# Two more weight slots and a column-grouped router in a hybrid encoder layer with 16 experts

## The chip, the cores and the metric

The kernel runs on one core of a Trainium2 chip. The metric is the device time of one execution in microseconds (us). A core has TensorE (matrix products, results in PSUM), VectorE, ScalarE and GpSimd (element-wise work), SyncE (here it issues nearly all transfers) and 16 DMA engines that move data between HBM and the core's SBUF. SBUF has 128 partitions; a slot of 8 KB in each of them holds 1 MB.

## The reference

One layer on 256 tokens of width 2048, all in float32. The first sub-layer is not changed. The second routes: each of 16 experts chooses the 32 tokens with the highest affinity to it.

```python
h = h + merged @ w_out[l]
h = h + expert_choice_ffn(rms_norm(h, ffn_norm_g[l]), w_router[l], w_gate_e[l], w_up_e[l], w_down_e[l])

def expert_choice_ffn(hn, w_router, w_gate_e, w_up_e, w_down_e):
    cap = CAPACITY_FACTOR * T // N_EXPERTS                      # 32
    aff = jax.nn.softmax((hn @ w_router).astype(jnp.float32), axis=-1)
    gate, idx = lax.top_k(aff.transpose(0, 2, 1), cap)
    xe = jax.vmap(lambda h, i: h[i])(hn, idx)
    hid = jax.nn.silu(einsum(xe, w_gate_e)) * einsum(xe, w_up_e)   # 2048 -> 1024
    ye = einsum(hid, w_down_e) * gate[..., None]                   # 1024 -> 2048
    out = zeros.at[idx].add(ye)
```

The expert weights are 3 x 16 x 2048 x 1024 x 4 bytes, 402.7 MB, of the 556 MB that the kernel moves.

## The kernel before

The order of the work is: normalisation of x; the input projection and the RWKV-7 heads, interleaved; the attention projections (`da`) and attention; the two branch projections (`br`), merged into mh and ml; the output projection (`w_out`); the routing; and four quarters of four experts each. Each engine runs its instructions in an order fixed at build time by a scheduler, which takes the program's order, priorities and a timing model; semaphores hold the engines together.

**Projections.** `wsplit` (L198) loads a chunk of weights of 0.5 MB into one of three raw buffers, ScalarE casts it to a high part wh (L205) and VectorE subtracts to a low part wl (L206), two buffers each. `project_t` (L213) multiplies: 12 matmuls of 512 columns for each chunk (L224 to L226). w_out is four blocks of 512 output columns, 8 chunks each, 32 chunks in all. A chunk's transfer is issued when the chunk three before it is split.

**The expert loads.** 384 loads of 1 MB stand in the list ew_loads, for every quarter 64 of gate and up weights and 32 of down weights, in the order in which they are used. `fetch` (L171) takes the next load and a slot from the pool that slot_of (L165) names, and issues its transfer on SyncE (L179). The slots: NEW = 14 form the ring, of which NE1 = 2 lie in pool ew1 (open since the attention projections) and 12 in ewa, opened ahead of w_out; NEB = 8 more (ewb, L887) are opened after the routing code and hold one load each, loads 14 to 21, until the first quarter's gate and up products are done; their place then goes to the accumulator acc. `pace` (L188), called with each chunk, issues one load for every PACE = 3 chunks while ring slots are free; a one-element GpSimd copy (L176) ties it to the chunk's split. What is left of the 14 goes out behind w_out (L831). All other loads wait for a slot that TensorE has done with.

**Memory.** Pools are stacked from the left and from the right end of SBUF. On the left, mg holds mh and ml (32 KB a partition) and wp the raw, wh and wl buffers; both are released after w_out, and ewb takes their place and more. On the right lie hres, ew1, ewa and, during w_out only, out2 (o2, L810) with hT and hsq. A pool that is opened over memory of an earlier one waits until that one's tiles are done with.

**Router logits.** For each w_out block, h is completed (L817), transposed in PSUM (pth, L821) and copied to hT (L822), 512 features by 256 tokens. Then 8 products with hT as the stationary operand (128x128) and 16 columns of wr as the moving one give the block's share of the logits, plg (L826), and VectorE adds it to lgt (L828, L830). A float32 product appears as two matmul records. After the last block come the norm (hrs), the softmax, the transposed affinities, four rounds of top-8, the one-hot matrices oh and ohr, the gather of the tokens (pxe, L906, xe, L907) and the first expert matmuls (pgu, L923): four experts at a time, each in its own group of 32 columns of the array. Down products are pd (L957).

Of the kernel before, what the change touches and what calls it, by code (L numbers as in the profile page):

```python
# [8 lines left out]
F32 = mybir.dt.float32  # L9
# [3 lines left out]
OP = mybir.AluOpType  # L13
AX = mybir.AxisListType
# [4 lines left out]
T = 256  # L19
# [5 lines left out]
NE = 16  # L25
# [7 lines left out]

GSCHED = (1, 4, 1, 4, 6)
PS, PCH = 9000, 16000
NEW, NE1, NEB = 14, 2, 8
PACE = 3

C_ID = 0
C_ROPE = C_ID + 128  # L40
# [12 lines left out]
def trunk_kernel(ctx, tc, x, attn_norm_g, w_in, q_norm_g, k_norm_g, lambda_q1, lambda_k1, lambda_q2,  # L53
# [3 lines left out]
    nc = tc.nc  # L57
    V, A, G, PE, SP = nc.vector, nc.scalar, nc.gpsimd, nc.tensor, nc.sync
    left = "left"
# [5 lines left out]
    lp = tc.alloc_tile_pool(name="lp", bufs=1, space=PSUM)  # L65
# [5 lines left out]
    @contextmanager  # L71
    def prio(base):
        old = tc.cur_priority
        if base > 0:
            tc.cur_priority = base
        yield
        tc.cur_priority = old if base > 0 else tc.cur_priority

    def misc(shape, name):
        return prepp.tile(shape, F32, name=name, tag="pr")  # L80

    cst = cp.tile([128, C_RW], F32, name="cst")
    ident = cst[:, C_ID:C_ID + 128]
# [68 lines left out]
    for q in range(4):  # L152
# [4 lines left out]
        for c0, w in pieces(q):  # L157
            n = 2048 // w
            for c in range(8 // n):
                for j in range(4):  # L160
                    ew_loads.append(w_down_e[0, 4 * q + j].rearrange("(p ft) n -> p ft n", ft=8)
                                    [:, n * c:n * c + n, c0:c0 + w])
    ew_state = dict(pools=[None, None, None], tiles=[], used=0, chunks=0)

    def slot_of(i):  # L165

        if NEW <= i < NEW + NEB:
            return 2
        return int((i if i < NEW else i - NEB) % NEW >= NE1)

    def fetch(after=None):  # L171
        i = len(ew_state["tiles"])
        pool = ew_state["pools"][slot_of(i)]
        w = pool.tile([128, 2, FF], F32, name="w", tag="w")
        if after is not None:
            G.tensor_copy(w[0:1, 0, 0:1], after)  # L176
        src = ew_loads[i]
        w = w.rearrange("p a f -> p (a f)").rearrange("p (a f) -> p a f", f=src.shape[2])
        SP.dma_start(w, src)  # L179
        ew_state["tiles"].append(w)  # L180
# [7 lines left out]
    def pace(wl):  # L188
# [4 lines left out]
        ew_state["chunks"] += 1  # L193
        if ew_state["chunks"] % PACE == 0:
            with prio(2000000 + ew_state["chunks"]):
# [446 lines left out]
    hres = tc.alloc_tile_pool(name="hres", bufs=1, side=right)  # L642
    hrow = hres.tile([128, 2, D], F32, name="h")
    fg = hres.tile([128, KT], F32, name="fg")
    wr = hres.tile([128, KT, NE], F32, name="wr")
    fg2 = hres.tile([16, 128], F32, name="fg2")
    ssb = hres.tile([128, 2, 4], F32, name="ssb")
    lgt = hres.tile([128, 2, NE], F32, name="lgt")
# [24 lines left out]
    with ExitStack() as es:  # L673
# [59 lines left out]
        for t in range(2):  # L733
            SP.dma_start(hrow[:, t], x[0, t * 128:(t + 1) * 128, :])
        SP.dma_start(fg, ffn_norm_g[0].rearrange("(p kt) -> p kt", kt=KT))
        SP.dma_start(wr, w_router[0].rearrange("(kt p) e -> p kt e", p=128))
        SP.dma_start(fg2, ffn_norm_g[0].rearrange("(a b) -> a b", b=128))
        for h in range(8):
# [23 lines left out]
            for t in range(2):  # L762
                for j in range(2):
                    PE.matmul(po[:, t], aT[:, j, t * 128:(t + 1) * 128], vt[:, j, h * 128:(h + 1) * 128],
                              start=j == 0, stop=j == 1)
# [42 lines left out]
    w_out_k = w_out[0].rearrange("(kt p) n -> p kt n", p=128)  # L808
    with ExitStack() as es:
        o2 = es.enter_context(tc.tile_pool(name="out2", bufs=2, side=right))  # L810
        for blk in range(4):
            cs = slice(blk * 512, (blk + 1) * 512)
            ps = project_t(w_out_k, KT, blk * 512, mh, ml, f"wo{blk}", (chp, "ch") if blk % 2 else None)
            hT = o2.tile([128, 4, T], F32, name="hT", bufs=1)
            hsq = o2.tile([128, 512], F32, name="hsq", bufs=1)
            for t in range(2):
                V.tensor_tensor(h[:, t, cs], ps[t], h[:, t, cs], op=OP.add)  # L817
                A.activation(hsq, h[:, t, cs], AF.Square, accum_out=ssb[:, t, blk:blk + 1])
                pt = misc([128, 4, 128], f"pth{blk}_{t}")
                for j in range(4):  # L820
                    PE.transpose(pt[:, j], h[:, t, blk * 512 + j * 128:blk * 512 + (j + 1) * 128], ident)  # L821
                A.copy(hT[:, :, t * 128:(t + 1) * 128], pt)  # L822
            pl = misc([128, 2, NE], f"plg{blk}")
            for t in range(2):
                for j in range(4):
                    PE.matmul(pl[:, t], hT[:, j, t * 128:(t + 1) * 128], wr[:, blk * 4 + j], start=j == 0, stop=j == 3)  # L826
            if blk == 0:
                V.tensor_copy(lgt, pl)  # L828
            else:
                V.tensor_tensor(lgt, pl, lgt, op=OP.add)  # L830
    while len(ew_state["tiles"]) < NEW:  # L831
        fetch()
    mg.release()
# [50 lines left out]


    with ExitStack() as es:
        ewb = tc.alloc_tile_pool(name="ewb", bufs=NEB, side=left)  # L887
        ew_state["pools"][2] = ewb
        for q in range(4):
            es_ = slice(4 * q, 4 * q + 4)  # L890

# [31 lines left out]
                                PE.matmul(pgu[2 * gu + hf][js], xe[kt // 4][:, kt % 4, js],  # L923
                                          wt[2 * j + gu][:, k, hf * 512:(hf + 1) * 512], start=kt == 0, stop=kt == KT - 1)
            if q == 0:
                ewb.release()
                e3 = es.enter_context(tc.tile_pool(name="e3", bufs=1, side=left))
                acc = e3.tile([128, 2, D], F32, name="acc")
            gT = e3.tile([128, T], F32, name="gT")
# [11 lines left out]
            hT = e3.tile([128, 8, 128], F32, name="hdT", bufs=1)  # L941
# [5 lines left out]
            for c0, cw in pieces(q):  # L947
# [3 lines left out]
                for c in range(8 // nft):  # L951
                    wt = [expert_w() for j in range(4)]
                    for k, nb, j in ([(k, 0, j) for j in range(4) for k in range(nft)] if nft == 8 else
# [4 lines left out]
                                          start=ft == 0, stop=ft == 7)  # L958
# [61 lines left out]
```

## Time and profile before

| what | value |
|---|---|
| three runs | 1873.23, 1873.61, 1876.11 us; median 1873.61 |
| the profiled execution | 1877.81 us, span of its instructions 1876.0 us |
| busy in the span | TensorE 1679.5 us (90%), its weight loads 1032.0, VectorE 701.4, ScalarE 440.4, GpSimd 189.9 |
| DMA | 556.48 MB, mean 297 GB/s |
| granted TensorE clock | 0.977 of full speed on average |

A row of the profile names the line of the kernel, the engine, the operation and the tiles (out<-in, with shapes as partitions x elements). PE is TensorE's matmuls, PEld its weight loads, SPq SyncE's queue of transfers. "idle before" is what the engine waited for ahead of the instruction. The chain of waits follows the work that ended last back to its start. A DMA share of 1 means that all 16 engines were busy; values a little over 1 occur. Some matmul records are missing from a trace, so counts of merged rows can be low.

### The profile page before, as it was taken

Reading aid. Unit: us, or ns where it says so; the run is one execution under the profiler, and the core shown is the slowest. Engines: PE = TensorE matmul, PEld = TensorE weight load, DVE = VectorE, ACT = ScalarE, POOL = GpSimd, SP = SyncE. Lnnn points to the kernel's source line nnn. Section 1 sums busy time; section 2 is a strip of 40 time slices with the busy share of each in tenths; the row PEclk is TensorE's granted clock in tenths of the full one; section 3 lists DMA queues with packets and bytes.
Section 4 is the critical chain, followed back from the end, with each engine's and each line's share of the span. In section 5 each row is a group of like instructions: output and inputs, shape, how many; then the busy total and the mean of one; then the engine's idle time right before and its main releaser. Section 6 shows DMA issues by size and latency. Waiting matters only on the chain.

```text
span 1876.0 us, 27452 instructions
## 1 busy us (share of the span) xinstructions
PE 1679.5 (90%) x11179; PEld 1032.0 (55%) x11179; DVE 701.4 (37%) x1524; ACT 440.4 (23%) x768; POOL 189.9 (10%) x295
## 2 busy tenths in 40 slices
PE   7999999998998999999989889888898888878878
PEld 6988898887996778998734222222222222211223
DVE  4678797877645667774410000000000000000000
ACT  6444443443434455444300000000000000000000
POOL 2342223322001331000000000000000000000000
PEclk9999999999999999999989999999999999999999
DMA  5655644554657565788799999999999999999997
GB/s 170 172 141 146 171 112 117 135 142 115 170 153 234 169 201 162 221 261 298 275 419 393 424 421 425 427 427 425 420 425 427 427 424 420 425 427 427 425 417 278
DMA packets 230382, 556.48 MB, mean 297 GB/s; under 512 B 40954, under 2 KB 138736, under 8 KB 197232
## 3 DMA queue, kind: packets, MB, share of 16 engines
q1 hardware_dynamic: 229904, 554.68, 79.8%
q8 instruction: 88, 1.44, 0.3%
q14 instruction: 38, 0.31, 0.0%
q0 software_dynamic: 352, 0.05, 0.0%
HBM read 543.14 MB, written 11.53 MB: 296 GB/s over the span
## 4 chain that ended last, share of the span: by engine, by line
DMA 35%; PE 27%; SPq 2%; DVE 1%; issue 1%; ACT 0%; POOL 0%; ACTq 0%; POOLq 0%; DVEq 0%
DMA w<-in_w_down_e_dram 13%; DMA w<-in_w_gate_e_dram 11%; DMA w<-in_w_up_e_dram 11%; PE pgu L923 6%; PE pd L957 4%; SPq L179 2%; PE pxe L906 2%; PE pc_br L242 2%; PE pc_br L244 2%; PE pj_wo L225 2%; PE pc_br L243 2%; PE pj_wo L226 2%; PE pj_wo L224 2%; PE pj_da L225 1%; PE pj_da L224 1%; PE pj_da L226 1%
## 5 line engine op out<-in xcount | busy, mean ns | idle before, releaser
L923 PE MATMUL pgu<-w,xe 128*32 128x512 f32 x2048 | 458.6, 610 | 63.4 <-DMA w<-in_w_gate_e_dram 31.6
L923 PEld LDWEIGHTS pgu<-w,xe 128*32 128x32 f32 x2048 | 111.9, 110 | 393.9 <-issue 232.6
L957 PE MATMUL pd<-w,hdT 128*32 128x512 f32 (+1 forms) x1088 | 246.3, 589 | 54.7 <-DMA w<-in_w_down_e_dram 53.8
L957 PEld LDWEIGHTS pd<-w,hdT 128*32 128x32 f32 x1088 | 65.2, 111 | 232.4 <-DMA w<-in_w_down_e_dram 122.3
L242 PE MATMUL pc_gt<-xh,wh_gt 128*128 128x256 f32 x512 | 149.9, 295 | 1.4 <-ACT wh_gt L205 1.4
L244 PE MATMUL pc_gt<-xh,wl_gt 128*128 128x256 f32 x512 | 145.6, 295 | 2.7 <-DVE wl_gt L206 2.5
L243 PE MATMUL pc_gt<-xl,wh_gt 128*128 128x256 f32 x512 | 148.0, 292 | 0.0
L938 ACT ACTIVATE th<-pgu 128x512 f32<-128x512 f32 x8 | 4.8, 597 | 522.1 <-PE pgu L923 522.1
L907 DVE TENSOR_TENSOR xe<-pxe,fg 128x512 f32<-128x512 f32 x16 | 11.0, 690 | 296.4 <-PE pgu L923 241.3
L242 PE MATMUL pc_rkv<-xh,wh_rkv 128*128 128x256 f32 x384 | 111.4, 293 | 1.0 <-ACT wh_rkv L205 1.0
L244 PE MATMUL pc_rkv<-xh,wl_rkv 128*128 128x256 f32 x384 | 108.1, 293 | 3.9 <-DVE wl_rkv L206 3.9
L243 PE MATMUL pc_rkv<-xl,wh_rkv 128*128 128x256 f32 x384 | 110.4, 290 | 0.0
L966 DVE TENSOR_TENSOR acc<-poe,acc 128x512 f32<-128x512 f32 (+1 forms) x26 | 16.9, 651 | 245.3 <-PE poe L965 245.3
L242 PEld LDWEIGHTS pc_gt<-xh,wh_gt 128*128 128x128 f32 x512 | 100.0, 195 | 4.6 <-ACT wh_gt L205 1.6
L243 PEld LDWEIGHTS pc_gt<-xl,wh_gt 128*128 128x128 f32 x512 | 100.1, 195 | 2.3 <-issue 1.2
L244 PEld LDWEIGHTS pc_gt<-xh,wl_gt 128*128 128x128 f32 x512 | 97.4, 195 | 6.1 <-DVE wl_gt L206 3.9
L939 DVE SCALAR_TENSOR_TENSOR th<-th,pgu 128x512 f32<-128x512 f32 x8 | 5.5, 688 | 252.0 <-ACT th L938 251.9
L206 DVE TENSOR_TENSOR wl_gt<-raw_gt,wh_gt 128x1024 fp32r<-128x1024 f32 x64 | 80.4, 1256 | 39.5 <-ACT wh_gt L205 39.3
L205 ACT CAST wh_gt<-raw_gt 128x1024 fp32r<-128x1024 f32 x64 | 67.0, 1046 | 92.8 <-PE pc_gt L243 75.8
L225 PE MATMUL pj_da<-wl_da,xh 128*128 128x512 f32 x192 | 77.8, 405 | 7.0 <-DVE wl_da L206 6.9
L961 ACT COPY ye<-pd 128x512 f32<-128x512 f32 (+1 forms) x17 | 9.5, 560 | 310.0 <-PE pd L957 310.0
L206 DVE TENSOR_TENSOR wl_da<-raw_da,wh_da 128x1024 fp32r<-128x1024 f32 x48 | 63.7, 1326 | 34.3 <-ACT wh_da L205 33.4
(385 smaller groups left out, 2868.0 us busy)
## 6 DMA issues: line engine op xcount, KB each, us to landing
w<-in_w_gate_e_dram SPq DMA_DIRECT2D x128, 1024.0 KB, 19.5
w<-in_w_up_e_dram SPq DMA_DIRECT2D x128, 1024.0 KB, 19.5
w<-in_w_down_e_dram SPq DMA_DIRECT2D x128, 1024.0 KB, 18.1
raw_gt<-in_w_in_dram SPq DMA_DIRECT2D x64, 512.0 KB, 3.8
raw_rkv<-in_w_in_dram SPq DMA_DIRECT2D x48, 512.0 KB, 3.8
raw_da<-in_w_in_dram SPq DMA_DIRECT2D x48, 512.0 KB, 3.6
raw_wo<-in_w_out_dram SPq DMA_DIRECT2D x32, 512.0 KB, 5.3
raw_br<-in_w_branch_b_dram SPq DMA_DIRECT2D x16, 512.0 KB, 4.1
```

The source lines that it names most:

```text
L179: SP.dma_start(w, src)
L205: A.copy(wh[:, :n], raw[:, :n])
L206: V.tensor_tensor(wl[:, :n], raw[:, :n], wh[:, :n].bitcast(F32), op=OP.subtract)
L224: PE.matmul(ps[t], lh[:, kt, s], wh[:, j], start=first, stop=False)
L225: PE.matmul(ps[t], lh[:, kt, s], wl[:, j], start=False, stop=False)
L226: PE.matmul(ps[t], ll[:, kt, s], wh[:, j], start=False, stop=last)
L242: PE.matmul(ps[c][:m], wh[:, j, cs], rh[:, kt], start=first, stop=False)
L243: PE.matmul(ps[c][:m], wh[:, j, cs], rl[:, kt], start=False, stop=False)
L244: PE.matmul(ps[c][:m], wl[:, j, cs], rh[:, kt], start=False, stop=last)
L906: PE.matmul(px[:, j], h[:, t, kt::KT], ohr[:, t], start=t == 0, stop=t == 1)
L923: PE.matmul(pgu[2 * gu + hf][js], xe[kt // 4][:, kt % 4, js], wt[2 * j + gu][:, k, hf * 512:(hf + 1) * 512], start=kt == 0, stop=kt == KT - 1)
L957: PE.matmul(pd[nb][js], hT[:, ft, js], wt[j][:, k, nb * nw:(nb + 1) * nw], start=ft == 0, stop=ft == 7)
```

## The change

Five edits:

- NEW becomes 16 and PACE 2: the ring has 16 slots (14 in ewa), and among the w_out chunks one load is issued for every two chunks.
- The 8 late slots come from two pools, 6 and 2, opened one after the other on the left; slot_of gives loads 16 to 21 to the first and 22 and 23 to the second.
- The DMA scratch, memory at the start of SBUF for the descriptors of transfers that GpSimd issues, is set to 2048 bytes a partition (default 16384).
- Router logits: the 16 columns of wr become the stationary operand and hT (256 tokens) the moving one. The four 128-feature pieces of a block go to four column groups of the array, that is to partitions 0, 32, 64 and 96 of one PSUM tile plg, and accumulate there over the four blocks. plg is zeroed first, since only 16 of each 32 partitions are written.
- At the end plg is copied to SBUF (lgs, in out2), multiplied with rsum (the identity summed over its four pieces, made once) so that the four groups are added and the result is transposed to tokens on partitions, and copied to lgt.

```diff
--- before.py
+++ after.py
@@ -33,8 +33,8 @@
 
 GSCHED = (1, 4, 1, 4, 6)
 PS, PCH = 9000, 16000
-NEW, NE1, NEB = 14, 2, 8
-PACE = 3
+NEW, NE1, NEB = 16, 2, (6, 2)
+PACE = 2
 
 C_ID = 0
 C_ROPE = C_ID + 128
@@ -160,13 +160,13 @@
                 for j in range(4):
                     ew_loads.append(w_down_e[0, 4 * q + j].rearrange("(p ft) n -> p ft n", ft=8)
                                     [:, n * c:n * c + n, c0:c0 + w])
-    ew_state = dict(pools=[None, None, None], tiles=[], used=0, chunks=0)
+    ew_state = dict(pools=[None, None, None, None], tiles=[], used=0, chunks=0)
 
     def slot_of(i):
 
-        if NEW <= i < NEW + NEB:
-            return 2
-        return int((i if i < NEW else i - NEB) % NEW >= NE1)
+        if NEW <= i < NEW + sum(NEB):
+            return 2 + (i >= NEW + NEB[0])
+        return int((i if i < NEW else i - sum(NEB)) % NEW >= NE1)
 
     def fetch(after=None):
         i = len(ew_state["tiles"])
@@ -643,6 +643,7 @@
     hrow = hres.tile([128, 2, D], F32, name="h")
     fg = hres.tile([128, KT], F32, name="fg")
     wr = hres.tile([128, KT, NE], F32, name="wr")
+    rsum = hres.tile([128, 32], F32, name="rsum")
     fg2 = hres.tile([16, 128], F32, name="fg2")
     ssb = hres.tile([128, 2, 4], F32, name="ssb")
     lgt = hres.tile([128, 2, NE], F32, name="lgt")
@@ -733,6 +734,7 @@
         for t in range(2):
             SP.dma_start(hrow[:, t], x[0, t * 128:(t + 1) * 128, :])
         SP.dma_start(fg, ffn_norm_g[0].rearrange("(p kt) -> p kt", kt=KT))
+        V.tensor_reduce(rsum, ident.rearrange("p (j e) -> p e j", j=4), axis=AX.X, op=OP.add)
         SP.dma_start(wr, w_router[0].rearrange("(kt p) e -> p kt e", p=128))
         SP.dma_start(fg2, ffn_norm_g[0].rearrange("(a b) -> a b", b=128))
         for h in range(8):
@@ -808,6 +810,9 @@
     w_out_k = w_out[0].rearrange("(kt p) n -> p kt n", p=128)
     with ExitStack() as es:
         o2 = es.enter_context(tc.tile_pool(name="out2", bufs=2, side=right))
+
+        plg = lp.tile([128, T], F32, name="plg", tag="L")
+        V.memset(plg, 0.0)
         for blk in range(4):
             cs = slice(blk * 512, (blk + 1) * 512)
             ps = project_t(w_out_k, KT, blk * 512, mh, ml, f"wo{blk}", (chp, "ch") if blk % 2 else None)
@@ -820,14 +825,14 @@
                 for j in range(4):
                     PE.transpose(pt[:, j], h[:, t, blk * 512 + j * 128:blk * 512 + (j + 1) * 128], ident)
                 A.copy(hT[:, :, t * 128:(t + 1) * 128], pt)
-            pl = misc([128, 2, NE], f"plg{blk}")
-            for t in range(2):
-                for j in range(4):
-                    PE.matmul(pl[:, t], hT[:, j, t * 128:(t + 1) * 128], wr[:, blk * 4 + j], start=j == 0, stop=j == 3)
-            if blk == 0:
-                V.tensor_copy(lgt, pl)
-            else:
-                V.tensor_tensor(lgt, pl, lgt, op=OP.add)
+            for j in range(4):
+                PE.matmul(plg[32 * j:32 * j + NE], wr[:, blk * 4 + j], hT[:, j], start=blk == 0, stop=blk == 3)
+        lgs = o2.tile([128, T], F32, name="lgs", bufs=1)
+        V.tensor_copy(lgs, plg)
+        pl = misc([128, 2, NE], "pl")
+        for t in range(2):
+            PE.matmul(pl[:, t], lgs[:, t * 128:(t + 1) * 128], rsum[:, 0:NE], start=True, stop=True)
+        V.tensor_copy(lgt, pl)
     while len(ew_state["tiles"]) < NEW:
         fetch()
     mg.release()
@@ -884,8 +889,8 @@
 
 
     with ExitStack() as es:
-        ewb = tc.alloc_tile_pool(name="ewb", bufs=NEB, side=left)
-        ew_state["pools"][2] = ewb
+        ewb = [tc.alloc_tile_pool(name=f"ewb{i}", bufs=n, side=left) for i, n in enumerate(NEB)]
+        ew_state["pools"][2:] = ewb
         for q in range(4):
             es_ = slice(4 * q, 4 * q + 4)
 
@@ -923,7 +928,8 @@
                                 PE.matmul(pgu[2 * gu + hf][js], xe[kt // 4][:, kt % 4, js],
                                           wt[2 * j + gu][:, k, hf * 512:(hf + 1) * 512], start=kt == 0, stop=kt == KT - 1)
             if q == 0:
-                ewb.release()
+                for z in ewb[::-1]:
+                    z.release()
                 e3 = es.enter_context(tc.tile_pool(name="e3", bufs=1, side=left))
                 acc = e3.tile([128, 2, D], F32, name="acc")
             gT = e3.tile([128, T], F32, name="gT")
@@ -1006,7 +1012,7 @@
     import concourse.tile as _tile
     from concourse.bass_utils import run_bass_kernel_spmd as _run
 
-    nc = _bacc.Bacc("TRN2", target_bir_lowering=False, num_devices=1)
+    nc = _bacc.Bacc("TRN2", target_bir_lowering=False, num_devices=1, dynamic_dma_scratch_size=2048)
     arrays, args = {}, []
     for name in _INS + ["consts"]:
         a = make_consts() if name == "consts" else _np.ascontiguousarray(inputs[name])
```

## Rows read from the trace of the kernel before

**Rows 1.** The page, 40 slices of the span: DMA share in tenths, GB/s

```profile
DMA  5655644554657565788799999999999999999997
GB/s 170 172 141 146 171 112 117 135 142 115 170 153 234 169 201 162 221 261 298 275 419 393 424 421 425 427 427 425 420 425 427 427 424 420 425 427 427 425 417 278
```

**Rows 2.** The page, the chain that ended last, shares of the span by engine

```profile
DMA 35%; PE 27%; SPq 2%; DVE 1%; issue 1%; ACT 0%; POOL 0%; ACTq 0%; POOLq 0%; DVEq 0%
```

**Rows 3.** Windows A:B: length, busy PE, PEld, DVE, ACT, POOL, PEclk, DMA share, GB/s

```profile
1015.00:1019.00 4.00, 4.00 (x36) 1.22 (x27) 0.00 (x0) 0.00 (x0) 0.00 (x0) 1.00 0.35 84
1019.00:1838.00 819.00, 693.49 (x2910) 198.11 (x2906) 39.38 (x60) 18.36 (x33) 0.00 (x0) 0.98 1.02 424
```

**Rows 4.** Windows of 2 us, same columns: one of the two empty ones

```profile
930.00:932.00 2.00, 1.98 (x15) 1.50 (x16) 0.67 (x2) 2.00 (x6) 0.15 (x1) 1.00 0.00 0
```

**Rows 5.** Timeline of SyncE's queue, 918 to 1140 us: start, length, what

```profile
919.55 2.30 SPq L179 DMA_DIRECT2D w<-in_w_up_e_dram  x2
...
933.45 0.33 SPq L179 DMA_DIRECT2D w<-in_w_gate_e_dram  x1
...
954.04 0.80 SPq L179 DMA_DIRECT2D w<-in_w_gate_e_dram  x2
```

**Rows 6.** What SyncE's queue waited for, 930 to 1060 us: total, times, longest

```profile
SPq L179 <- PE pgu L923: 66.0, 15, 15.9
...
SPq L179 <- PE plg L826: 6.6, 1, 6.6
```

**Rows 7.** Chain of waits in order of time, the end: start, length, what

```profile
1824.29 13.65 DMA w<-in_w_down_e_dram
...
1859.43 11.45 PE pd L957 x64
```

**Rows 8.** Chain of waits in order of time, w_out and routing

```profile
863.11 1.69 PE plg L826 x16
...
887.61 1.69 PE plg L826 x16
...
932.31 1.08 PE plg L826 x8
```

**Rows 9.** Chain of waits in order of time, the first expert quarter

```profile
949.58 14.73 PE pgu L923 x128
...
968.79 7.06 PE pgu L923 x52
...
975.85 1.50 PE pxe L906 x6
```

**Rows 10.** Windows in w_out, columns as in group 3

```profile
850.00:875.00 25.00, 24.98 (x122) 20.37 (x121) 11.60 (x12) 10.62 (x14) 0.35 (x2) 1.00 0.83 298
875.00:900.00 25.00, 25.00 (x124) 21.06 (x123) 11.10 (x11) 10.86 (x15) 0.52 (x3) 1.00 0.79 278
```

**Rows 11.** The w_out chunks (tile raw_wo): durations ns, waits for it, landing

```profile
L205 ACT CAST wh_wo<-raw_wo x32: 1030/1055/1055, 831.1 to 924.4; 128x1024 fp32r<-128x1024 f32 x32
...
L206 DVE TENSOR_TENSOR wl_wo<-raw_wo,wh_wo x32: 1219/1226/1226, 832.2 to 925.5; 128x1024 fp32r<-128x1024 f32 x32
...
  PEld pj_wo L225: 1.0, 3
...
DMA to landing us min/median/max: 4.0/5.3/7.1
```

**Rows 12.** Timeline of VectorE in the routing, 929 to 950 us

```profile
933.42 0.19 DVE L830 TENSOR_TENSOR lgt<-plg,lgt 128x32 f32<-128x32 f32 x1 [0.24 <-PE plg L826]
...
934.51 0.16 DVE L94 SCALAR_TENSOR_TENSOR hrs<-rh_t,hrs 128x2 f32<-128x2 f32 x1
...
937.14 0.41 DVE L858 COPY wk<-paf 16x256 f32<-16x256 f32 x1 [0.69 <-PE paf L855]
```

**Rows 13.** The parameter rows (tile rows): the transpose, and landing

```profile
L309 PE MATMUL pprm<-cst,rows x1: 251/251/251, 28.0 to 28.0; 100*128 100x100 f32 x1
...
DMA to landing us min/median/max: 4.9/5.7/6.1
```

## The prediction

> **What bounds the kernel now.** I read the page's slices first [rows 1]. In the first 20 of 40 the DMA engines are 40 to 80% busy; from the 21st on their share is 9 tenths or more and they move 420 to 427 GB/s in nearly all of them. The shares of the chain of waits say the same: transfers make up 35% of the span, TensorE 27% [rows 2]. In the stretches of the compute half that I cut out TensorE is busy all the time [rows 10]. So the kernel is a compute half followed by a stream of 384 expert loads of 1 MB, and the end is set by when that stream becomes dense and by how much of it is already in SBUF then.
>
> The table by stretches gives the size of this [rows 3]: from 1019 to 1838 us the DMA share is 1.02 at 424 GB/s, which is full. One load is 1.0486 MB, so 1.0486 / 0.424 = **2.47 us**. Ahead of 1019 us the stream has two holes. The first is while the routing starts: in the two slices of 2 us from 930 to 934 us not a byte moves [rows 4]. SyncE tells why: the 14th load is issued at about 921 us, the 15th only at 933.45 us [rows 5], and its wait is put down to the router's matmuls (plg, 6.6 us) [rows 6]. The late slots (ewb) lie over memory that the out2 pool still holds, and plg reads its hT. The second hole is at 1015 to 1019 us (share 0.35, so 0.65 x 4 = 2.6 us): the stream is out of free slots and waits for TensorE's expert matmuls [rows 3, 6].
>
> Between the holes lies the step that decides. The eight late loads need 19.8 us from 933.45, so the 22 slots are full at 953.2 us or a little later, and the next load is issued at 954.04 us, when TensorE, at work on expert products since 949.58 us [rows 9], has let go of the first slots [rows 5]. From there on every load has a place in a line: the end is that release plus (384 minus the slots) loads plus the hole at 1015. At the end of the kernel TensorE takes over: behind the transfer that ends at 1824.29 + 13.65 = 1837.94 us it computes the last pieces without waiting for another, and its last expert matmul ends 32.9 us later, at 1870.88 [rows 7]. These pieces move with the stream.
>
> **The change part by part.**
>
> *Two more slots.* At the first release 24 loads can be in SBUF instead of 22; two loads less have to follow it: 2 x 2.47 = **4.95 us**. Are the two there in time? They are issued among the w_out chunks (PACE 2: 14 in 28 chunks, the last at chunk 27 of 32), and the stream has room: the first hole lies behind them. In steady state the ring of 16 instead of 14 gives nothing, since the share is full already.
>
> *The late slots in two pools.* Six may now go out when mg is free, at the last w_out matmul, two when out2 is. That matmul ends at 929.4 us: the last split starts at 925.5 and takes 1.23 us [rows 11], and a chunk's matmuls follow, 2.72 us (24.5 us a block, less 1.69 for plg and about 1 for the transposes, by 8). By the line above this is worth almost nothing by itself: eight loads from 929.6 us would be in at 949.4 us or a little later, and the stream would then wait for the same release at 954 us. Its worth is that it covers the slots against a later end of out2. I cost it at 0; without this cover the price is what out2 ends later, 0.5 us by the sum below.
>
> *Router logits.* Before, each block has 8 calls (16 records) at 1.69 us on the chain of waits, and blocks follow at 24.5 us (863.11, 887.61; the next likewise), with TensorE at 100% [rows 8, 10]. After, there are 4 calls, by the same count 8 records of 128x256, in four column groups. No row shows this form. The expert matmuls have the four groups with twice the columns: 128 records in 14.73 us, 0.115 us each, so 8 cost 0.92 us if half the columns bring nothing, 0.46 us if they halve it [rows 9]. If the groups did not overlap, the 256-column records at the end give 11.45 / 64 = 0.179 us, 1.43 us for 8 [rows 7]. I take **0.70 us**, the middle of the two nearest. Three blocks lie ahead of the end of w_out: 3 x (1.69 - 0.70) = **2.97 us** earlier (0.78 to 3.69).
>
> What a switch between the column groups and the whole array costs can be bounded: the expert run between two gathers, 52 records in 7.06 us, stands 1.08 us over the pace of 0.115 us, if no record is missing; and the gather follows it without a gap, 968.79 + 7.06 = 975.85 [rows 9]. I take 0, for the missing gap. The Trainium skill, "TensorEngine Tiling (Array Packing)", section Key Properties, speaks against the edit: a change of tiling mode drains TensorE. As an estimate by "TensorE: Matmul & The Clock Gate", section "Single matmul latency" (about 0.175 us for a drain), six switches would cost 1.05 us and the sum below would end at 1869.2 us; no row here shows a drain by itself.
>
> *PACE 2, and what the loads meet.* The same 32 w_out chunks now share the DMA engines with a load for every two chunks, not three. Per pair of chunks TensorE needs (24.5 - 0.99) / 4 = 5.88 us. For the DMA: from 850 to 900 us the shares 0.83 and 0.79 make 40.5 us, at a full share of 1.02 39.7 us, for 14.4 MB [rows 10]. With a load for every three chunks, 3 x 24.5 / 8 = 9.19 us apart, 5.44 loads lie in it, 5.70 MB and 13.4 us; the rest, 8.70 MB, is 16.6 chunks of 0.524 MB in 26.3 us, 1.58 us each. A pair with its load is 2.47 + 3.16 = **5.63 us**. It fits, with 4% left; at PACE 3 it was 7.21 in 9.19 us, 22%. So chunks will land later. They took 4.0 to 7.1 us, median 5.3, and TensorE's weight loads lost 1.0 us to late splits [rows 11]. With three buffers, three chunks need landing + cast 1.06 + split 1.23 + about 0.2 us: 7.8 us at the median against 3 x 2.72 = 8.16 us of matmuls, 9.6 us at 7.1. Ends: 0, and (9.6 / 3 - 2.94) x 28 = 7.3 us if each chunk landed like the worst. I take **2.0 us**, twice what was lost at the lighter load. So w_out ends 2.97 - 2.0 = 0.97 us earlier (6.5 later to 3.7 earlier). Queued behind a late chunk are ScalarE's cast, VectorE's split, and on SyncE the next chunk and the next load.
>
> *The tail of the logits.* Before, half of the last block's matmuls run while the second half of hT is copied; the other half follows at 932.31 us, and lgt is added at 933.42 [rows 8, 12]. After, all four calls wait for that copy: 932.31 + 0.70, then a copy of 256 columns out of PSUM (0.41 us as wk's), two calls (four records, half of 1.08 us), a copy (0.19) and three hand-overs: lgt at 934.3, its maximum at 934.5. Beside it runs VectorE's chain for hrs, ready only at 934.67 (934.51 + 0.16) [rows 12]; the new copy stands in its queue. So it costs **0.5 us** (0 to 1.5). The memset of plg and the sum for rsum are two short VectorE operations ahead of this stage, hidden under TensorE's 100%: 0; without cover about 0.4 us each.
>
> *Smaller DMA scratch.* It serves only GpSimd's own queue: the parameter rows of the start, each landed within 6.1 us, and the transpose that reads them is at 28.0 us [rows 13]. Cover of more than one landing: 0; without it, one landing (6 us) for each transfer that would have to wait for another.
>
> *Sum.* First release 0.97 - 0.5 = 0.47 us earlier, plus 4.95: **5.4 us**. The profiled execution took 1877.81 us, 1.8 over its span and 4.2 over the median of the three runs (1873.61); it would come to 1872.4, and the median to **1868.2 us**. The hole at 1015 stays as it is: the 49th load takes the place of the 47th, two transfers later and for the same release.
>
> **The rivals.**
>
> *The second hole goes.* The order of TensorE's expert matmuls and gathers there comes from a plan made at build time, and another plan may release earlier: -2.6 us, 1865.6. For it: the change gives the planner other pools and slots; against: TensorE's work there is the same.
>
> *The second hole grows.* The same plan may put off the release by the two loads: 4.95 lost, 1873.1. This is also the case in which the slots do not do what they are for.
>
> *The switches cost.* 1.08 us for each block's group, 3.2 us for the three: 1871.4. For it stands the slower run in rows 9, against it the missing gap.
>
> *Chunks land like the worst.* 7.3 us lost in w_out: 4.95 - (7.3 - 2.97) - 0.5 = 0.1, 1873.5.
>
> *Slower: w_out becomes DMA-bound.* If the mixed traffic is not capable of more than the 298 GB/s it moved from 850 to 875 us [rows 10], a pair (2.097 MB) takes 7.04 us against 24.5 / 4 = 6.13 before; 14 pairs, 12.8 us later: 1873.6 + 12.8 + 0.5 - 4.95 = 1882.0. It decides above 6.71 us a pair, below 313 GB/s (the loss of 8.2 us that makes 0.2%, over 14 pairs, on 6.13). Against it: those 298 GB/s went with a share of 0.83, so full is 298 x 1.02 / 0.83 = 366 GB/s. The Trainium skill, "DMA: Bandwidth & Descriptors", section "Issuing engines are not separate DMA queues", has all transfers interleave on the same 16 engines; the later landings beside a load agree.
>
> **How the numbers follow.** Forecast 0.50, second hole gone 0.14, worst landings 0.14, second hole grown 0.09, DMA-bound 0.08, switches 0.05. The forecast's own range is 1864.5 to 1871.5. The range is 1863.5 to 1876.0: it takes in all but the DMA-bound case and the ends where the hole goes and the router gains all of 3.7 us. A measurement of this kernel can tell about 0.2%, 3.7 us, from no change. Faster by more: 0.50 + 0.14, less 0.04 for the forecast's slow end, 0.60; within it: 0.14 + 0.09 + 0.05 and 0.03 of that end, 0.31; slower: 0.08 and the last 0.01.
>
> **What would show it.** On SyncE's queue: 14 loads among the w_out chunks, then six at the last w_out matmul, two at the end of out2, the next at about 953.5 us. Windows: w_out's share above 0.9, no byte for some 5 us ahead of that release. plg: 8 records per block, 0.5 to 0.9 us. The first transfers behind 1019 us should stand two loads ahead. It is wrong if w_out's last matmul comes after 929.4 us, if the first expert matmul comes after 949.6 us, or if the hole at 1015 changes by more than 1 us.

## The result and the profile after

The changed kernel took 1893.47 us in the median of four runs (1890.54 to 1899.66), the kernel before 1874.86 us beside it: a ratio of 1.0097 (95% interval 1.0082 to 1.0113). I had forecast 1868.2 us and a range up to 1876.0. The change is slower, by 18.6 us in the medians.

The profiled execution took 1893.63 us, with a span of 1891.9 us, 15.9 more than before. The page's slices show the same picture as [rows 1], with other heights: full from the 23rd slice on, but at 409 to 422 GB/s up to the 38th.

```profile
DMA  5555634554657555689798999999999999999998
GB/s 176 171 142 148 169 108 117 142 141 117 167 154 232 173 189 175 222 275 342 299 383 372 414 409 419 421 421 416 410 418 422 421 417 409 417 422 420 419 402 273
```

Windows of the changed kernel (length, busy time of PE, PEld, DVE, ACT and POOL, granted clock, DMA share, GB/s): w_out [rows 10], the second hole and the stream [rows 3].

```profile
850.00:875.00 25.00, 24.29 (x113) 18.66 (x112) 11.89 (x11) 10.60 (x14) 0.69 (x4) 1.00 0.95 345
1015.00:1023.00 8.00, 8.00 (x42) 4.70 (x44) 0.00 (x0) 0.00 (x0) 0.00 (x0) 1.00 0.33 136
1019.00:1838.00 819.00, 672.57 (x2902) 191.85 (x2902) 37.55 (x58) 18.38 (x33) 0.00 (x0) 0.96 1.01 414
```

Three things differ from the forecast. The stream moves 414 GB/s where it moved 424, at a share of 1.01 against 1.02; from 1060 us on, clear of the hole, it is 416 GB/s at 1.02. The hole is 5.4 us long (0.67 of 8 us) where it was 2.6. And in w_out TensorE is no longer busy all the time. The transfers of w_out (tile raw_wo), and who waited for their casts and splits (us in total, times) [rows 11]:

```profile
  PEld pj_wo L225: 6.0, 8
  PE pj_wo L225: 2.9, 6
  PEld pj_wo L224: 1.0, 3
...
DMA to landing us min/median/max: 3.7/6.4/8.5
```

SyncE's queue (start, length, what), against [rows 5]: six late loads at the last w_out matmul and two behind the copy of the logits, as meant; then the first release at 956.52 us, 2.5 later than before, and a load that ends the second hole at 1022.07 us (before: 1016.80).

```profile
932.26 0.34 SPq L179 DMA_DIRECT2D w<-in_w_gate_e_dram  x1
...
936.61 0.33 SPq L179 DMA_DIRECT2D w<-in_w_gate_e_dram  x1
...
956.52 0.81 SPq L179 DMA_DIRECT2D w<-in_w_gate_e_dram  x2
...
999.70 0.33 SPq L179 DMA_DIRECT2D w<-in_w_up_e_dram  x1
1022.07 0.33 SPq L179 DMA_DIRECT2D w<-in_w_gate_e_dram  x1
```

The logits are what I took them for: 8 records in 0.62 us, shown with the products of w_out around them, and at the end two short calls.

```profile
864.03 0.61 PE L224 MATMUL pj_wo<-wh_wo,mh 128*128 128x512 f32 x2
864.58 0.62 PE L829 MATMUL plg<-hT,wr 128*16 128x256 f32 x8
865.13 0.50 PE L225 MATMUL pj_wo<-wl_wo,mh 128*128 128x512 f32 x1
...
935.92 0.62 PE L834 MATMUL pl<-rsum,lgs 128*128 128x16 f32 x4 [0.55 <-DVE lgs L831]
```

At the end of the kernel TensorE's own work stands behind the last transfers as in [rows 7]: the transfer of 14.56 us ends at 1853.80 us, the last expert matmul 33.0 us later (32.9 before).

```profile
1839.24 14.56 DMA w<-in_w_down_e_dram
...
1875.38 11.45 PE pd L963 x64
```

**The theory.** SBUF pools are stacked, and the new tile rsum (32 floats, 128 bytes a partition) stands in hres, ahead of ew1 and ewa on the right. It moves every ring slot down by 128 bytes: in the built programs the slots of before begin at multiples of 256 bytes, those of after 128 past one. Theory: this costs each row of a transfer some time. Rivals: the ring's size, the smaller scratch, or the order of the issues.

### The profile page after: what moved, and what is told of

It is laid out like the page before. It is cut to its first block, busy times and chain, and to the rows that moved or that the text cites. A ratio compares the mean times of both kernels' runs of the same rounds, so it can differ in the third digit from the quotient of the medians.

```text
span 1891.9 us, 27406 instructions
## 1 busy us (share of the span) xinstructions
PE 1663.3 (88%) x11151; PEld 1019.3 (54%) x11151; DVE 703.5 (37%) x1524; ACT 440.1 (23%) x768; POOL 192.3 (10%) x299
## 4 chain that ended last, share of the span: by engine, by line
DMA 41%; PE 19%; SPq 3%; DVE 2%; ACT 1%; issue 1%; POOL 0%; ACTq 0%; DVEq 0%; POOLq 0%
DMA w<-in_w_gate_e_dram 22%; DMA w<-in_w_down_e_dram 12%; DMA w<-in_w_up_e_dram 4%; PE pgu L928 3%; PE pd L963 3%; SPq L179 3%; DMA raw_wo<-in_w_out_dram 2%; PE pc_br L242 2%; PE pc_br L244 2%; PE pc_br L243 2%; PE pxe L911 1%; PE pj_da L225 1%; PE pj_da L224 1%; PE pj_da L226 1%; DVE wl_wo L206 1%
## 5 line engine op out<-in xcount | busy, mean ns | idle before, releaser
L928 PE MATMUL pgu<-w,xe 128*32 128x512 f32 x2048 | 453.7, 609 | 71.8 <-DMA w<-in_w_gate_e_dram 53.3
L963 PE MATMUL pd<-w,hdT 128*32 128x512 f32 (+1 forms) x1088 | 236.3, 614 | 74.1 <-DMA w<-in_w_down_e_dram 73.1
## 6 DMA issues: line engine op xcount, KB each, us to landing
w<-in_w_gate_e_dram SPq DMA_DIRECT2D x128, 1024.0 KB, 19.8
w<-in_w_up_e_dram SPq DMA_DIRECT2D x128, 1024.0 KB, 19.8
```

The source lines that it names most:

```text
L963: PE.matmul(pd[nb][js], hT[:, ft, js], wt[j][:, k, nb * nw:(nb + 1) * nw], start=ft == 0, stop=ft == 7)
```

## The experiments

This table puts all runs on the same stages, read from the timelines of PE and SyncE: the length of w_out (first to last matmul), the time from there to the first pgu, from there to the issue that ends the second hole (the 47th load with 14 slots, the 49th with 16; at 16 slots and PACE 3 the same load is taken, though no hole is left there), and from there to the end of the span. "Past" is where the ring slots begin, in bytes past a multiple of 256. The medians are of 4 runs (10 for e2, e3, e7, e8 and e9), with the interval of the ratio to the kernel before (1874.86 us for after, 1875.98 for e1, e2, e3 and e5, 1875.52 for e6 to e9, 1875.69 for the other four).

| kernel | past | slots | PACE | logits | w_out | to pgu | to hole's end | to the end | median, ratio |
|---|---|---|---|---|---|---|---|---|---|
| before | 0 | 14 | 3 | old | 96.0 | 19.8 | 67.2 | 859.2 | |
| after | 128 | 16 | 2 | new | 97.8 | 20.0 | 69.9 | 869.8 | 1893.5, 1.0082 to 1.0113 |
| e1_pad128 | 128 | 14 | 3 | old | 95.8 | 19.7 | 66.4 | 874.5 | 1892.2, 1.0073 to 1.0107 |
| e5_pad32 | 224 | 14 | 3 | old | 95.7 | 19.7 | 66.4 | 875.1 | 1894.9, 1.0092 to 1.0123 |
| e4_pad224 | 32 | 14 | 3 | old | 96.0 | 19.8 | 67.2 | 876.5 | 1895.9, 1.0086 to 1.0120 |
| e3_scratch | 0 | 14 | 3 | old | 96.6 | 19.8 | 67.1 | 858.8 | 1875.0, 0.9985 to 1.0004 |
| e2_aligned | 0 | 16 | 2 | new | 99.2 | 19.9 | 69.9 | 853.5 | 1876.6, 0.9993 to 1.0017 |
| e9_all | 0 | 16 | 2 | new | 100.2 | 20.0 | 69.3 | 854.9 | 1876.8, 0.9999 to 1.0020 |
| e7_slots | 0 | 16 | 2 | old | 100.4 | 19.8 | 70.9 | 854.1 | 1876.8, 0.9997 to 1.0019 |
| e8_router | 0 | 14 | 3 | new | 93.6 | 19.7 | 66.7 | 858.4 | 1874.9, 0.9978 to 1.0002 |
| e6_pace3 | 0 | 16 | 3 | new | 93.8 | 19.9 | 63.5 | 855.7 | 1865.1, 0.9929 to 0.9962 |
| e11_slots3 | 0 | 16 | 3 | old | 95.7 | 19.8 | 63.0 | 854.8 | 1867.1, 0.9936 to 0.9966 |
| e12_onepool | 0 | 16 | 3 | new | 93.6 | 20.0 | 63.4 | 855.6 | 1865.6, 0.9928 to 0.9958 |
| e10_all3 | 0 | 16 | 3 | new | 92.6 | 19.8 | 63.1 | 855.1 | 1865.2, 0.9930 to 0.9964 |

What stands ahead of w_out is nearly the same code in all of them, and yet its first matmul came between 829.7 and 837.9 us. So single spans scatter by some us, and the stages say more than they do.

### Where the ring lies

e1: the kernel before, moved by 128 bytes.

```diff
     lgt = hres.tile([128, 2, NE], F32, name="lgt")
+    hpad = hres.tile([128, 32], F32, name="hpad")
+    V.memset(hpad, 0.0)
```

> The kernel before with one tile of 128 bytes per partition (zeroed once, read by nobody) added to the pool hres, which moves the 14 ring slots of the expert weights down by 128 bytes, from addresses that are multiples of 256 to addresses 128 past one; slots, queue order, logits and scratch stay. Theory A (the stream of after is slower because its ring slots lie 128 bytes past a multiple of 256): the steady stream from 1060 to 1838 us goes at about 416 GB/s instead of 424, gate/up stretches at 421 and down stretches at 409, and the end comes about 16 us later: 1891. Rival B (the stream is slower because of 16 slots, the smaller scratch or the order of the issues): no difference, 424 GB/s, 1875.

e2: the kernel after, moved back.

```diff
-    rsum = hres.tile([128, 32], F32, name="rsum")
+    rsum_ = hres.tile([128, 64], F32, name="rsum")
+    rsum = rsum_[:, 0:32]
```

> The kernel after with the tile rsum taken as 256 bytes per partition instead of 128 (its first 128 are used), which puts the 16 ring slots back on multiples of 256; all else as after. Theory A (alignment): the stream is at 424 GB/s again, 427 in gate/up and 420 in down stretches, and of the 18 us some 16.5 come back: about 1877. Rival B (slots, scratch, order of issues): stays at 1893 with 416 GB/s. By either, the w_out stage still ends about 2.8 us later than before and the hole near 1018 us is still about 3 us longer.

e3: the kernel before with the smaller scratch alone.

```diff
-    nc = _bacc.Bacc("TRN2", target_bir_lowering=False, num_devices=1)
+    nc = _bacc.Bacc("TRN2", target_bir_lowering=False, num_devices=1, dynamic_dma_scratch_size=2048)
```

> The kernel before with the smaller DMA scratch alone; the ring slots keep their addresses modulo 256, the memory that is freed stays unused. Theory A (alignment of the ring): no difference, 1875 within 2 us, 424 GB/s. Rival B1 (the scratch: descriptors of SyncE's transfers share it, or the rows of the start wait for room in it): the stream at 416 GB/s and about 1891, or the first transpose of the parameter rows later than 28 us.

e5 and e4: as e1, with hpad of 8 and of 56 floats (32 and 224 bytes).

> The kernel before with a tile of 32 bytes per partition added to hres, which puts the 14 ring slots 224 bytes past a multiple of 256; all else as before. Theory A in the form that only the count of pieces a row is cut into at 256-byte lines matters: the same as 128 bytes past, about 16 us, 1891. Theory A in the form that the bytes of the first piece matter (a first piece of 32 bytes costs more than one of 128): by the Trainium skill, DMA: Bandwidth & Descriptors, section How a descriptor splits into AXI transactions, 7 more beats on 256 for a row of 8 KB and on 128 for one of 4 KB, as an estimate 2.7% and 5.5% of the load time, some 30 us, 1905. Rival B (not the alignment): 1875.

> The kernel before with a tile of 224 bytes per partition added to hres, which puts the 14 ring slots 32 bytes past a multiple of 256 (128 past cost 16.2 us, 224 past 19.0 us); all else as before. Theory A1 (every place off the 256-byte lines costs one more piece a row, whatever its size): 416 GB/s and 16 to 19 us again, 1892 to 1895. Theory A2 (the bytes of the first and last piece count, in steps of 32): one more step on 256 for a row of 8 KB, on 128 for one of 4 KB, as an estimate by the Trainium skill, DMA: Bandwidth & Descriptors, section How a descriptor splits into AXI transactions: 0.4% and 0.8% of the loads' time, about 4 us, 1880. The run 224 past spoke against A2 (30 us expected of it, 19 measured).

Measured: e1 is 16.2 us slower than the kernel before, with nothing but 128 bytes more in hres; e2 is within the measurement of it; e3 too. The theory stands, the rivals fall. The windows show it in one line each, the long stretch and then 20 us of down and of gate/up loads. Before:

```profile
1060.00:1838.00 778.00, 656.50 (x2738) 185.80 (x2737) 38.69 (x59) 18.36 (x33) 0.00 (x0) 0.98 1.02 424
1100.00:1120.00 20.00, 17.60 (x74) 5.01 (x73) 2.77 (x4) 1.17 (x2) 0.00 (x0) 1.00 1.03 421
1180.00:1200.00 20.00, 18.19 (x82) 7.05 (x80) 0.69 (x1) 0.00 (x0) 0.00 (x0) 1.00 1.01 426
```

e1, 128 bytes past:

```profile
1060.00:1838.00 778.00, 649.87 (x2700) 180.99 (x2698) 38.54 (x59) 18.37 (x33) 0.00 (x0) 0.98 1.02 416
1100.00:1120.00 20.00, 17.39 (x72) 4.69 (x71) 2.76 (x4) 1.17 (x2) 0.00 (x0) 1.00 1.03 410
1180.00:1200.00 20.00, 18.02 (x80) 7.05 (x80) 0.69 (x1) 0.00 (x0) 0.00 (x0) 1.00 1.01 420
```

e2, the kernel after on multiples of 256 again:

```profile
1060.00:1838.00 778.00, 640.11 (x2742) 181.81 (x2738) 38.66 (x59) 18.39 (x33) 0.00 (x0) 0.96 1.02 424
```

e5, 224 past, and e4, 32 past:

```profile
1060.00:1838.00 778.00, 647.55 (x2692) 179.68 (x2690) 35.90 (x55) 17.19 (x31) 0.00 (x0) 0.98 1.02 416
```

```profile
1060.00:1838.00 778.00, 649.02 (x2691) 181.03 (x2692) 35.91 (x55) 17.84 (x33) 0.00 (x0) 0.98 1.02 416
1100.00:1120.00 20.00, 17.39 (x72) 4.66 (x71) 2.76 (x4) 1.17 (x2) 0.00 (x0) 1.00 1.02 409
1180.00:1200.00 20.00, 18.06 (x80) 7.03 (x80) 0.69 (x1) 0.00 (x0) 0.00 (x0) 1.00 1.01 419
```

The share is 1.02 in all of them: the engines are as busy, and a load takes longer. How far past hardly matters: 32, 128 and 224 all give 416 GB/s, and the three intervals of the ratio overlap. So theory A2 (the bytes count) falls and A1 stands.

### What PACE 2 does to w_out and to the second hole

e6: e2 with PACE 3.

```diff
-PACE = 2
+PACE = 3
```

> The kernel after with the 256-byte rsum (ring slots on multiples of 256) and PACE 3 as before instead of 2: 16 slots and the new logits, but a load for every three w_out chunks; the loads that this leaves go out at the end of w_out. The plan of TensorE's order is made anew and comes out a little different. Theory A (what is left of the loss, beside the alignment, is w_out starved by the denser loads: its last matmul at 932.2 us instead of the 926.4 us that the cheaper logits would allow; and the end is counted from the second hole, so only a release there that is earlier than 1016.8 + 2 x 2.47 us gains): w_out share 0.80 again and no wait of TensorE on the split above 1 us, last w_out matmul at about 926.5, first expert matmul at about 946.7, the issue that ends the second hole at about 1014 to 1016 us, time about 1868 to 1870. Rival B (the loss of w_out comes from the column groups, not from the loads): w_out still ends near 932 and the time stays near 1877.

e7: e2 with the old logits (plg, lgs and the product with rsum are gone again).

```diff
-                PE.matmul(plg[32 * j:32 * j + NE], wr[:, blk * 4 + j], hT[:, j], start=blk == 0, stop=blk == 3)
+                    PE.matmul(pl[:, t], hT[:, j, t * 128:(t + 1) * 128], wr[:, blk * 4 + j], start=j == 0, stop=j == 3)
```

> The kernel after with the 256-byte rsum and the old router logits (8 calls of 16 weight columns a block): two more slots, two late pools and PACE 2 alone. Theory A (PACE 2 makes w_out wait for its chunks): w_out's blocks have 0.99 us more of TensorE work each, part of which only fills the wait for chunks: last w_out matmul between 932.2 and 935.2 us, the issue that ends the second hole between 1022 and 1025, time 1877 to 1880, 1 to 4 us behind the kernel before although two more loads are in SBUF. Rival B (as I predicted: PACE 2 costs 2.0 us): last w_out matmul at 931.4, time about 1871 to 1872.

e9: e2 with 32 bytes of padding in the const pool and 96 in the pool route, both on the left.

```diff
+    cpad = cp.tile([128, 8], F32, name="cpad")
+    V.memset(cpad, 0.0)
...
+    rpad = rt_.tile([128, 24], F32, name="rpad")
+    V.memset(rpad, 0.0)
```

> The kernel after with the 256-byte rsum, and 32 and 96 bytes of padding in the left stack, so that the buffers of the streamed weights (raw, 224 bytes past a multiple of 256 so far) and the eight late slots (128 past) lie on multiples of 256 as well; PACE 2. Theory A (the buffers' place costs DMA time wherever a transfer is long): w_out's chunks land earlier and TensorE loses less to late splits, some 2 of the 5.8 us: time about 1874 to 1875 against 1876.6. Rival B (chunks of w_out come with other row lengths, and what they wait for is the loads beside them): same as with the ring aligned alone, 1876.6. Should the first half of the kernel, with its shares of 0.4 to 0.8, end earlier too, transfers were on its path.

Measured: e6 is 10.5 us faster than the kernel before, and 11.6 faster than e2, which differs in PACE alone. Theory A holds in the main, and the gain is larger than it said. The share from 850 to 875 us is 0.84 instead of 0.94 in e2, and w_out is 5.4 us shorter (99.2 to 93.8), and the release that ended the hole comes another 6.4 us sooner (69.9 to 63.5), of which 2.2 are given back (853.5 to 855.7), since the queue still holds transfers then. In e6 the wait of TensorE's weight loads for the splits is down to 2.0 us (e2 7.3, the expectation at most 1), and the median landing of a w_out chunk to 5.5:

```profile
  PEld pj_wo L225: 2.0, 4
  PE pj_wo L225: 0.5, 1
...
DMA to landing us min/median/max: 3.6/5.5/7.5
```

e7 tells that the denser loads cost w_out 4.4 us with the old logits too (96.0 to 100.4), where I had put 2.0. Its time is that of the kernel before, 1876.8 us, so at PACE 2 the two slots gain nothing, and rival B (1871 to 1872) falls. Nor do the new logits gain there: e2, which has them, took 1876.6. e9 gained nothing in w_out (100.2 against 99.2), so there the place of the buffers isn't what the chunks wait for; rival B stands.

The hole needs a look at TensorE's order, which is made at build time and comes out different when PACE changes. Timeline of PE in the kernel after, from the first expert matmul to the hole's end (pgu runs only; between them lie the gathers pxe):

```profile
952.19 14.61 PE L928 MATMUL pgu<-w,xe 128*32 128x512 f32 x128 [0.36 <-DVE xe L912]
...
1000.23 1.90 PE L928 MATMUL pgu<-w,xe 128*32 128x512 f32 x4
...
1002.69 1.90 PE L928 MATMUL pgu<-w,xe 128*32 128x512 f32 x4
...
1008.21 1.90 PE L928 MATMUL pgu<-w,xe 128*32 128x512 f32 x4
...
1013.73 1.90 PE L928 MATMUL pgu<-w,xe 128*32 128x512 f32 x4
...
1019.25 11.06 PE L928 MATMUL pgu<-w,xe 128*32 128x512 f32 x88
```

The same in e6, the last runs ahead of its 49th load at 1010.20 us:

```profile
994.58 1.91 PE L929 MATMUL pgu<-w,xe 128*32 128x512 f32 x4
...
1000.10 1.92 PE L929 MATMUL pgu<-w,xe 128*32 128x512 f32 x8
...
1005.63 15.82 PE L929 MATMUL pgu<-w,xe 128*32 128x512 f32 x120
```

A run of 128 records takes 0.114 us a record, one of 4 takes 0.475: in the program those 4 are two calls with the weights of one load, and a load belongs to one expert, which has its own column group; so one column group works while three stand idle. After has four of these runs ahead of the hole's end, e6 one. Up to the last run shown, after needed 67.1 us for 280 records and e6 58.9 us for 268; the six gathers between are the same work, and the pgu runs alone take 43.4 and 36.3 us (eight and seven runs, summed). So TensorE, busy nearly all the time in both, comes to the release of the 49th load 6.4 us sooner in e6 (63.5 against 69.9). Then the stream doesn't run dry: e6 has a share of 1.02 from 1005 to 1010 us and of 0.98 from 1010 to 1015.

```profile
1010.00:1015.00 5.00, 5.00 (x46) 1.80 (x46) 0.00 (x0) 0.00 (x0) 0.00 (x0) 1.00 0.98 385
```

Why the scheduler orders them so isn't settled, and no run changed PACE with the order held fixed. That the time lies in the order, and not in TensorE's speed or a wait, is read from these rows: the granted clock is 0.99 in both stretches, and TensorE is idle for 1.6 us of the 67.1 and 0.8 of the 58.9.

### The parts alone

e8: the kernel before with the new logits alone (rsum as in e2): the edit of e7, the other way round.

> The kernel before with the new router logits alone (rsum taken as 256 bytes, so that the ring slots stay on multiples of 256): 14 slots, one pool of eight late slots, PACE 3. Theory A (the column groups give what their records show, 0.62 us for 1.69 a block, and the tail costs nothing): last w_out matmul about 3 us earlier than before, at 926.4, first expert matmul at about 946.6, all releases 3 us earlier, time about 1873 (3 us faster). Rival B (a switch of TensorE between the column groups and the whole array costs what the records do not show): less than 1 us earlier, 1875.

e11: e7 with PACE 3. e10: e9 with PACE 3. e12: e6 with one pool:

```diff
-NEW, NE1, NEB = 16, 2, (6, 2)
+NEW, NE1, NEB = 16, 2, (8,)
```

> The kernel after with the 256-byte rsum, PACE 3 and the old router logits: 16 slots and two late pools alone, at the old pace. By the stages measured so far (w_out 96.0 us long with the old logits at PACE 3, 93.8 with the new; 19.8 us from its end to the first expert matmul; 63.5 us from there to the 49th load with the plan of order that PACE 3 gives, which this kernel has too): all 2.2 us later than with the new logits, time about 1867. Rival (the gain of 10.5 us came from the logits' shorter path, without which the second hole comes back): 1871 or more.

> The kernel after with the 256-byte rsum and PACE 3, its eight late slots in one pool instead of two: all eight wait for the end of out2 (the copy of the logits out of PSUM) instead of six for the last w_out matmul. Theory A (as I predicted: the two pools are cover, worth nothing while the stream waits for the first release anyway): the eight loads are issued from 931.6 us on instead of 926.8, a hole of about 2 us at about 930, full at about 951.5, the first release at 950.9 as before, time within 2 us of the 1865.1 with two pools. Rival B (at PACE 3 the DMA engines are full from 917 us on and the second hole is gone, so every hole ahead of the stream counts in full): 2 to 3 us slower, 1867 to 1868.

> The kernel after with PACE 3 and every long transfer's target on multiples of 256: the 16 ring slots (256-byte rsum), the eight late slots and the buffers of the streamed weights (32 and 96 bytes of padding in the left stack). Theory A (a place off the lines costs DMA time only where transfers set the pace): the eight late loads are 0.27 us shorter in all, w_out's chunks wait for nothing at PACE 3; time 1864 to 1865, the same as with the ring alone aligned. Rival B (the first half waits for its streamed weights too): earlier by 2 us or more, w_out begins before 829 us.

Measured: e8 shortens w_out by 2.4 us (96.0 to 93.6) and keeps the tail at 19.7 us; its median is 0.6 us lower, with an interval that takes in no change and 2.4 us expected by its stages, so this time stays unclear. In its trace TensorE waits 1.9 us for splits, in before 1.0. e11, the slots and pools alone, is 8.6 us faster than the kernel before: 4.4 of it are the two loads (859.2 to 854.8 behind the hole) and 4.2 the release that comes sooner (67.2 to 63.0). e6 with the new logits is 2.0 us ahead of e11, near the 1.9 of its shorter w_out. e12 issues its eight loads at 930.30 us instead of 926.81 and loses 1.0 us of DMA time there (share 0.80 over 5 us), but its first release comes no later relative to the first pgu (4.0 us behind it, e6 4.2), and the time is 1865.6: cover and no more, as predicted.

```profile
930.00:935.00 5.00, 0.81 (x4) 0.24 (x3) 2.94 (x14) 0.88 (x4) 0.00 (x0) 0.50 0.80 293
```

e10 is the same as e6 in time. The 18.0 us from 1875.5 (the kernel before beside e6 to e9) to 1893.5 are thus put together from runs: slots and pools at PACE 3 -8.6 (e11), logits -2.0 (e6 against e11), PACE 2 +11.6 (e2 against e6), 128 bytes +16.8 (after against e2), in sum +17.8. These prices hold in this order only, for the parts lean on each other: with the old logits PACE 2 costs 9.7 us (e7 against e11), and the logits' 2.0 are 0.2 at PACE 2 (e2 against e7) and 0.6, not clear of noise, in e8.

## Why the prediction was wrong, point by point

**A load costs 2.47 us before and after**: this step failed. I took the stream's price from [rows 3] and carried it over as if it belonged to the chip; it belongs to the place of the slots as well, and 128 bytes past it is 1.0486 / 0.416 = 2.52 us. The working never added up what rsum moves, though the code gives it: 32 floats in a pool that the ring is stacked on. The place of the slots behind the hole costs 16.3 us (869.8 against 853.5 in e2), three quarters of the 21.3 us between the forecast of the span, 5.4 less, and the measured 15.9 more. By the stages the others are 2.8 in w_out and 2.7 up to the hole's end, the two next points, 0.6 ahead of w_out, and about 1 the other way.

**w_out at PACE 2**: mechanism right, term too small. I put 2.0 us between ends of 0 and 7.3; it was 4.4 (e7 against before) to 5.4 (e2 against e6). My pair of chunks needed 5.63 us of DMA in 5.88, and I took 4% of room for nearly enough. The share went to 0.95, the landings from 5.3 to 6.4 us, and that was enough for TensorE to wait 6.0 us for splits.

**The hole at 1015 us stays**: this step failed too. I counted the end from the first release and added a hole of constant length. But the later hole's release sets the stream, not the first one: in before its end is 67.2 us behind the first pgu, in after 69.9, in e6 63.5. I named both other cases as rivals (the hole goes, the hole grows) with 2.6 and 4.95 us; after is of the second kind, with 2.7 us, and e6 of the first. That the plan could change I gave 0.23 in all; in these runs each change of PACE, and that of the slots at PACE 3, came with another order.

**Two more slots are worth two loads**: right, 4.95 us worked out, 4.4 to 5.7 behind the hole at equal places (859.2 against 854.8 and 853.5). They show in the time only where the release ahead of them doesn't come later: in e11, not in e7.

**Logits**: 0.70 us a block, measured 0.62; 2.97 us for three blocks, measured 2.4 in e8 and 3.4 in e10, where TensorE waits only 0.5 us for splits; tail 0.5 us, measured -0.1 to 0.2. The 52 records in 7.06 us of [rows 9], which I read as a possible price of switching, are runs of partly filled column groups; no record of pgu was missing. The price of a switch is small. In before the products of w_out around the logits begin 2.16 us apart:

```profile
862.49 0.62 PE L224 MATMUL pj_wo<-wh_wo,mh 128*128 128x512 f32 x2
...
864.65 0.48 PE L225 MATMUL pj_wo<-wl_wo,mh 128*128 128x512 f32 x1
```

In after they begin 1.10 us apart (864.03 and 865.13 above), and without logits between them 0.45. So a block's logits cost 0.65 us instead of 1.71. At the pace of the expert matmuls, 0.114 us for twice the columns, the 8 records would take 0.46; what is left, 0.2 us a block, is the most that the two switches can have cost by this estimate.

**Late pools at 0, scratch at 0**: right (e12, at PACE 3, and e3).

My test in advance named the last w_out matmul after 929.4 us, the first expert matmul after 949.6 and a hole that changes by more than 1 us as signs that it is wrong. All three came true (932.2, 952.19, 2.8 us), but none of them names the largest part.

## What to carry to other kernels

When a tile is added to a stacked pool, add up its bytes and see where the targets of the long transfers come to lie: this kernel, whose end is set by transfers, paid 16 to 20 us for slots off multiples of 256 bytes, and 128 bytes of padding won it back. Where the order of an engine's work is made at build time, an edit of pace or slots can bring a new order; read the last hole ahead of the dense stream, not the first, and take its release from the new plan's runs. And don't count a stage as covered because the sum of its transfers fits: here a share of 0.95 cost 4.4 to 5.4 us.

## What the runs showed of the hardware

The cost of a target off a multiple of 256 bytes is nearly the same for each row of a transfer, not for each byte. Gate and up loads (128 rows of 8 KB by their shapes) went from 426 to 420 GB/s, 2.461 to 2.497 us: 0.035 us x 16 engines / 128 = 4.4 ns a row. Down loads (256 rows of 4 KB) went from 421 to 410 GB/s, 2.491 to 2.558 us: 0.067 x 16 / 256 = 4.2 ns a row. For the 208 and 128 loads behind the hole that makes 7.3 + 8.6 = 15.9 us, against 15.3 to 17.3 measured in the stages. (It counts 16 down loads of the last quarter, which have shorter rows, like the others.) The traces' records of single packets say the same: from 1060 to 1838 us a packet of 8 KB (one row) took 309.3 ns on average before, and 313.9, 314.9 and 315.0 with the slots 128, 32 and 224 bytes past (e1, e4, e5); one of 4 KB took 159.2, and 163.6, 163.4 and 163.6.

The Trainium skill, "DMA: Bandwidth & Descriptors", section "How a descriptor splits into AXI transactions", says that a piece of a transfer that doesn't begin at a multiple of 256 bytes starts its first transaction at the boundary below, and that the unused bytes are fetched and paid too. The traces agree on the multiple of 256, shown here for the SBUF side, to which these transfers write. For that side they don't agree that the unused bytes are paid: 32 bytes past should cost the least by it and 224 the most, and both give 416 GB/s. The Trainium skill speaks there of fetching, and the runs don't test the side that is read.

This is the size of the effect and its condition; which part of the path from HBM to SBUF pays it, the runs don't tell, and the source's place was not varied.

The other thing not expected: a product in one column group alone goes at a quarter of the pace of four side by side, 0.475 us a record of 512 columns against 0.114, and in after the planned order has four such runs ahead of the hole's end.
